# mLSTM by head with transposed scores: running maxima in rows through DRAM, denominators from ones columns, and a PSUM bank for each map's scores

## The chip, the cores and the metric

The kernel runs on one core of a Trainium2 chip. The metric is the device time of one execution in microseconds, and lower is better. Before the change the median of three runs is 1639.16 us (1638.51 to 1639.63).

## What is computed

One layer of an encoder for 272 tokens (16 meta tokens and 256 of input) with 2048 channels, in float32. One projection of the normalised input feeds three mixers (a short gated convolution A, an mLSTM of 4 heads B, a differential attention of 4 heads C) and their gates; the gated sum is projected and added to the input; a convolutional feed-forward block of 5632 channels follows. The change touches B and C only. The mLSTM, cut to what matters (q, k and v have 256 channels a head):

```python
b = jnp.cumsum(lfc, axis=-1)                        # log forget gates, summed
D = b[..., :, None] - b[..., None, :] + lic[..., None, :]
D = jnp.where(tri, D, -jnp.inf)
inter = b + m[..., None]
m_t = jnp.maximum(jnp.max(D, axis=-1), inter)       # running maximum
w = jnp.exp(D - m_t[..., None])
s = jnp.einsum('bhtd,bhsd->bhts', qc, kc) * w
num = g[..., None] * jnp.einsum('bhed,bhtd->bhte', C, qc) + jnp.einsum('bhts,bhse->bhte', s, vc)
den = g * jnp.einsum('bhd,bhtd->bht', n, qc) + jnp.sum(s, axis=-1)
h = num / jnp.maximum(jnp.abs(den), jnp.exp(-m_t))[..., None]
```

Both kernels compute it without chunks, as one causal map of 272 keys by 258 queries for each head. After it each head is RMS-normalised, scaled by a sigmoid gate, and projected. The differential attention takes, for each head, two softmax maps of 64 channels each and subtracts one from the other.

## The kernel before, in words

All large products are one **stream**: 537 slabs of 8 weight blocks (128x128) each come from DRAM in a fixed order (`Stream`). SyncE loads a slab into one of 5 raw buffers, ScalarE rounds it to `w_hi` (L187), VectorE makes the rest `w_lo` (L188), and TensorE multiplies each block three times (L273 to L275, called stream matmuls here). The split pair has 4 buffers; the split runs 3 slabs ahead of TensorE (`ahead=3`).

Everything else is **background**: generators that are advanced by one step (to their next `yield`) at each slab, which is a **tick**. The order in which engines get the instructions comes from the program's order and a scheduler's list; each engine then takes them in order. The background of differential attention is `diff_gen` (one generator a head), that of the mLSTM is `gates_gen` (once) and `ml_gen` (one a head and a query tile).

`QTILES` cuts the queries into tiles of 2, 128 and 128 (i = 0, 1, 2), which see 16, 144 and 272 keys. `KTILES` cuts the keys into 16, 128 and 128, `DTILES` into 100, 86 and 86. `ml_gen` makes, for one tile, the log weights of all keys by a matmul that selects the head's row from `crow` (L686), the scores with queries on the partitions (L689), maximum and mask in one VectorE instruction, the exponential on ScalarE, the product with its row sum, a transposition of the weighted scores to keys (L423), the product with v in three float32r matmuls a key tile (L710 to L712), and the transposition of the normalised result (L723). v itself is transposed to tokens at L433. `gates_gen` makes the gate columns (L632, L633, L639), the log sigmoid on [128, 12] tiles, and the running sums by matmuls with constant matrices (L666, L669, L674). `diff_gen` makes the scores at L484: the first map reads partitions 0 to 63, the second 64 to 127; the two maps of tile 2 have a bank each, those of tiles 1 and 0 share one bank (`shared`). Its other matmuls are L515, L525 and L537.

A float32 matmul stands in the trace as two records (two passes); a transposition and a float32r matmul as one.

Of the kernel before, what the change touches and what calls it, by code (L numbers as in the profile page):

```python
# [10 lines left out]
F32 = mybir.dt.float32  # L11
# [55 lines left out]
def _constants():  # L67
# [6 lines left out]
    for i, (q0, nq, nk) in enumerate(QTILES):  # L74
        t = q0 + np.arange(nq)[:, None]
        s = np.arange(nk)[None, :]
        put(f"mlm{i}", np.concatenate([np.zeros((nq, 1)), np.where(s <= t, 0.0, NEG)], 1).astype(np.float32))
        cid = lambda a: np.where(a < NMETA, 0, 1 + (a - NMETA) // 64)
        put(f"dam{i}", np.where(cid(s) <= cid(t), 0.0, NEG).astype(np.float32))
        for k, (k0, n) in enumerate(KTILES):  # L80
            if k0 >= nk:
                continue
            tt = k0 + np.arange(n)[:, None]
            ss = np.arange(-1, nk)[None, :]
            a = (tt <= ORIGIN[i]).astype(np.float32) - (tt <= ss).astype(np.float32)
            put(f"nt{i}_{k}", a)
    sel = np.zeros((NH, NH, 128), np.float32)
    for h in range(NH):
        sel[h, h] = 1.0
    put("sel", sel.reshape(NH, -1))  # L90
# [5 lines left out]
for _n, _w in (("g_mix", KT), ("g_ffn", KT), ("g_f", KT), ("conv_a", 12), ("ml_norm", 8), ("da_norm", 1),  # L96
               ("conv_f", 3 * FT), ("conv_fb", FT), ("b_if", 8), ("lam", 256)):
# [107 lines left out]
def encoder_layer_kernel(ctx: ExitStack, tc, xT, wst, wif, vecs, eye, consts, outT):  # L205
# [29 lines left out]
    nact = [1]  # L235
# [174 lines left out]
    def token_copy(v3, n, dst, lo=None):  # L410

        for a, b in ((slice(0, 16), slice(0, 1)), (slice(0, P), slice(1, n)))[: 1 if n == 1 else 2]:
            S.copy(dst[a, b], v3[a, b])
            if lo is not None:
                V.tensor_tensor(lo[a, b], v3[a, b], dst[a, b].bitcast(F32), op=ALU.subtract)

    def transpose_keys(src, nk, nq, dst, lo=None):

        ps = bank()
        n = 0  # L420
        for j, (k0, m) in enumerate(KTILES):
            if k0 < nk:
                T.transpose(ps[:m, j * P : j * P + nq], src[:nq, k0 : k0 + m], ident[:nq, :nq])  # L423
                n += 1
        v3 = ps[:, 0 : 3 * P].rearrange("p (j q) -> p j q", j=3)
        token_copy(v3[:, :, :nq], n, dst[:, :, :nq], None if lo is None else lo[:, :, :nq])
        return n

    def to_tokens(src, dst, lo=None):

        ps = bank()
        for j, (k0, m) in enumerate(KTILES):
            T.transpose(ps[:m, j * P : (j + 1) * P], src[:, k0 : k0 + m], ident)  # L433
        token_copy(ps[:, 0 : 3 * P].rearrange("p (j q) -> p j q", j=3), 3, dst, lo)

# [12 lines left out]
    def dv_put(vt, h):  # L448
# [4 lines left out]
        key_copy(dv[h], ps, 1)  # L453

# [15 lines left out]
    def diff_gen(h):  # L470
# [150 lines left out]
    lif = mix.tile([P, 3, 8], F32, name="lif")  # L621
    crow = [mix.tile([NH, 1 + q[2]], F32, name=f"crow{i}") for i, q in enumerate(QTILES)]
    nb = mix.tile([P, 3, NH], F32, name="nb")

    def gates_gen():
        split(wif2[:, :, 0:8], wif2[:, :, 8:16], wif_raw)
        V.tensor_tensor(eye2, ident[:16, 0:8], ident[:16, 8:16], op=ALU.add)
        V.memset(lif, 0.0)
# [8 lines left out]
        ps = bank()  # L637
        for j, (k0, m) in enumerate(KTILES):
            T.matmul(ps[:m, 8 * j : 8 * j + 8], lr[:, k0 : k0 + m], eye2, start=True, stop=True)  # L639
            V.tensor_tensor(lif[:m, j, :], ps[:m, 8 * j : 8 * j + 8], vs("b_if", 0, 8)[:m], op=ALU.add)  # L640
        f = lif[:, :, 4:8]
        y = small.tile([P, 3, 4], F32, tag="lsy", name="lsy")
        z = small.tile([P, 3, 4], F32, tag="lsz", name="lsz")
        z2 = small.tile([P, 3, 4], F32, tag="lsz2", name="lsz2")
# [284 lines left out]
```

## Time and profile before

| | before |
|---|---|
| median of 3 runs | 1639.16 us (1638.51 to 1639.63) |
| profiled execution, its own time | 1639.1 us |
| its span, first to last instruction | 1637.3 us |
| TensorE matmul busy | 99% of the span, 11948 records |
| VectorE busy | 62% |
| ScalarE busy | 45% |
| DMA | 53% of sixteen engines, 178 GB/s |

The span leaves 1.8 us around it. The busy times of the profile overlap where instructions are pipelined, so a TensorE instruction's own duration is its latency; what it costs the stream is read from the starts in the timeline.

### The profile page before, as it was taken

What the parts mean: (1) busy time and instruction counts of PE and PEld (TensorE: products, weight loads), DVE (VectorE), ACT (ScalarE), POOL (GpSimd) and SP (SyncE); (2) the same over time, 40 slices, a digit from 0 to 9 for tenths busy, and PEclk for the clock granted to TensorE, in tenths of its full rate; (3) what the DMA queues carried; (4) which work ended last, traced back from release to release, by engine and by line L of the source; (5) the groups of instructions that cost most, each with busy time, mean ns of one, the idle gap of its engine ahead of it and who ended that gap; (6) DMA issues with size and microseconds to landing.
All of it is one profiled execution on the core that took longest, in us unless ns stands there. A gap on an engine that the chain in (4) does not pass through costs nothing.

```text
span 1637.3 us, 29082 instructions
## 1 busy us (share of the span) xinstructions
PE 1618.4 (99%) x11948; PEld 1535.6 (94%) x11948; DVE 1007.7 (62%) x1594; ACT 738.4 (45%) x1067; POOL 46.6 (3%) x53
## 2 busy tenths in 40 slices
PE   8999999999999999999999999999999999999997
PEld 8999999899999999999999999999889999999886
DVE  6566555555555655656666777766556677676554
ACT  6445434344455544444444444444333444444442
POOL 0000000000000000000110000000000000000121
PEclk9999999999999999999999999999999999999998
DMA  8444555444444455555665555555555555555552
GB/s 318 150 155 146 179 181 181 146 151 155 142 147 150 160 183 192 185 181 180 201 207 177 181 189 183 185 189 182 192 185 189 181 185 188 183 188 183 191 183 90
DMA packets 83974, 291.03 MB, mean 178 GB/s; under 512 B 9344, under 2 KB 14080, under 8 KB 83712
## 3 DMA queue, kind: packets, MB, share of 16 engines
q1 hardware_dynamic: 82448, 287.91, 53.0%
q8 instruction: 93, 1.52, 0.4%
q10 hardware_dynamic: 1392, 1.26, 0.2%
q14 instruction: 41, 0.34, 0.1%
HBM read 287.03 MB, written 2.10 MB: 177 GB/s over the span
## 4 chain that ended last, share of the span: by engine, by line
PE 98%; issue 1%; DVE 0%; DMA 0%; ACT 0%; POOL 0%; POOLq 0%; ACTq 0%; DVEq 0%
PE ps L273 22%; PE ps L274 22%; PE ps L275 21%; PE ps L289 20%; PE ps L290 10%; PE ps L689 0%; PE ps L484 0%; PE ps L710 0%; PE ps L525 0%; PE ps L686 0%; DVE h L885 0%; DMA x_sb<-in_xT 0%; PE ps L515 0%; PE ps L712 0%; PE ps L711 0%
## 5 line engine op out<-in xcount | busy, mean ns | idle before, releaser
L187 ACT CAST w_hi<-w_raw 128x1024 fp32r<-128x1024 f32 (+1 forms) x537 | 562.7, 1048 | 813.8 <-issue 316.3
L188 DVE TENSOR_TENSOR w_lo<-w_raw,w_hi 128x1024 fp32r<-128x1024 f32 (+1 forms) x537 | 656.2, 1222 | 429.8 <-ACT w_hi L187 426.1
L273 PE MATMUL ps<-uhl,w_hi 128*128 128x258 f32 (+2 forms) x1664 | 482.2, 290 | 7.1 <-ACT w_hi L187 7.1
L274 PE MATMUL ps<-uhl,w_hi 128*128 128x258 f32 (+2 forms) x1664 | 476.3, 286 | 0.0
L275 PE MATMUL ps<-uhl,w_lo 128*128 128x258 f32 (+2 forms) x1664 | 473.5, 285 | 0.0
L273 PEld LDWEIGHTS ps<-uhl,w_hi 128*128 128x128 f32 x1664 | 314.3, 189 | 9.5 <-ACT w_hi L187 7.1
L274 PEld LDWEIGHTS ps<-uhl,w_hi 128*128 128x128 f32 x1664 | 315.6, 190 | 0.7
L275 PEld LDWEIGHTS ps<-uhl,w_lo 128*128 128x128 f32 x1664 | 314.4, 189 | 0.3
L289 PE MATMUL ps<-fhl,w_hi 128*128 128x512 f32 x704 | 252.2, 397 | 0.0
L289 PE MATMUL ps<-act,w_hi 128*128 128x512 f32 x682 | 237.5, 394 | 0.0
L274 PE MATMUL ps<-fhl,w_hi 128*128 128x258 f32 x704 | 199.7, 284 | 0.0
L273 PE MATMUL ps<-fhl,w_hi 128*128 128x258 f32 x704 | 198.8, 282 | 0.0
L275 PE MATMUL ps<-fhl,w_lo 128*128 128x258 f32 x704 | 197.5, 280 | 0.0
L290 PE MATMUL ps<-fhl,w_lo 128*128 128x256 f32 x704 | 189.9, 280 | 0.0
L290 PE MATMUL ps<-act,w_lo 128*128 128x256 f32 x682 | 187.6, 282 | 0.0
L289 PEld LDWEIGHTS ps<-fhl,w_hi 128*128 128x128 f32 x704 | 132.4, 188 | 28.3
L289 PEld LDWEIGHTS ps<-act,w_hi 128*128 128x128 f32 x682 | 126.1, 188 | 26.9
L274 PEld LDWEIGHTS ps<-fhl,w_hi 128*128 128x128 f32 x704 | 133.2, 189 | 2.1
L290 PEld LDWEIGHTS ps<-fhl,w_lo 128*128 128x128 f32 x704 | 133.2, 189 | 1.8
L275 PEld LDWEIGHTS ps<-fhl,w_lo 128*128 128x128 f32 x704 | 134.2, 191 | 0.0
L273 PEld LDWEIGHTS ps<-fhl,w_hi 128*128 128x128 f32 x704 | 132.4, 188 | 0.0
L290 PEld LDWEIGHTS ps<-act,w_lo 128*128 128x128 f32 x682 | 128.2, 188 | 3.0
(233 smaller groups left out, 1555.8 us busy)
## 6 DMA issues: line engine op xcount, KB each, us to landing
w_raw<-in_wst SPq DMA_DIRECT2D x535, 512.0 KB, 3.3
xr<-in_xT SPq DMA_DIRECT2D x16, 129.0 KB, 3.8
x_sb<-in_xT SPq DMA_DIRECT2D x7, 272.0 KB, 6.6
cst<-in_consts SPq DMA_DIRECT2D x1, 1252.5 KB, 6.6
out<-h SPq DMA_DIRECT2D x4, 256.0 KB, 3.1
out<-h ACTq DMA_DIRECT2D x3, 256.0 KB, 3.2
w_raw<-in_wst SPq DMA_DIRECT2D x2, 256.0 KB, 4.8
x_sb<-in_xT ACTq DMA_DIRECT2D x2, 136.0 KB, 3.1
```

The lines of the kernel that those rows point to most:

```text
L187: self.nc.scalar.copy(hi[:, a], raw[:, a])
L188: self.nc.vector.tensor_tensor(lo[:, a], raw[:, a], hi.bitcast(F32)[:, a], op=ALU.subtract)
L273: T.matmul(o, wh, xh[:, k, c0:c1], start=start, stop=False)
L274: T.matmul(o, wh, xl[:, k, c0:c1], start=False, stop=False)
L275: T.matmul(o, wl, xh[:, k, c0:c1], start=False, stop=stop)
L289: one = lambda: T.matmul(o, wh, xhl[:, k, :, a:b], start=(k == 0), stop=(k == K - 1))
L290: two = lambda: T.matmul(o[:, : b - a], wl, xhl[:, k, 0, a:b], start=False, stop=False)
```

## The change

- **Gates in rows.** `gates_gen` keeps the gates of the four heads as rows [4, 272]: two matmuls (L635, L636 of the changed kernel), the log sigmoid on [4, 272] tiles, the running sum and the running maximum by doubling steps on VectorE. Three rows go to DRAM from ScalarE's queue (`crow`, `nrow`, `erow`) and come back: as columns `ccol` and `ecol` (one element a packet), and per head as `w`, a row broadcast to 128 partitions.
- **mLSTM by head.** `ml_gen` runs once a head. The scores are made transposed, keys on the partitions, in three key tiles of 100, 86 and 86 (`DTILES`); only queries from 0, 86 and 172 on are made for them. So the transposition of weighted scores goes. The result is made in three query tiles of 86 (`MQ`), from 1, 2 and 3 key tiles. v has two more columns (ones in the high part), whose product is the denominator.
- **v and the result.** Both halves of a head's v are transposed in one step (`mv_evac`), and so is the result of all queries.
- **Differential attention.** The two maps of a head have a bank each for all three query tiles, and the six score matmuls are issued one after the other, before the first VectorE instruction on them.
- **Order of the background.** One generator runs at a time (`nact` is gone).

```diff
-        ("mlm0", 17), ("mlm1", 145), ("mlm2", 273),
-        ("dam0", 16), ("dam1", 144), ("dam2", 272),
-        ("nt0_0", 17), ("nt1_0", 145), ("nt1_1", 145),
-        ("nt2_0", 273), ("nt2_1", 273), ("nt2_2", 273),
-        ("sel", NH * 128),
+        ("dam0", 16), ("dam1", 144), ("dam2", 272), ("causal", PW),
...
     def tick():
...
-            i = 0
-            g = background[i]
-            background.remove(g)
+            g = background.popleft()
             try:
                 next(g)
-                background.insert(min(nact[0] - 1, len(background)), g)
+                background.appendleft(g)
...
+    def mv_evac(h, j):
...
+                for ks in ((0,), (1, 2)):
+                    m = DTILES[ks[0]][1]
+                    ps = bank()
+                    for n, k in enumerate(ks):
+                        for i in range(2):
+                            c = n * 256 + i * P
+                            T.transpose(ps[:m, c : c + P], vt[:, i, DTILES[k][0] : DTILES[k][0] + m], ident)
...
+                    split(hi, lo, src)
...
     def diff_gen(h):
-        pm = {}
-        shared = None
+        pm, sc = {}, {}
+        pair, col = [bank(), bank()], 0
         for i, (q0, nq, nk) in reversed(list(enumerate(QTILES))):
             a = q0 - SKIP
-            if i < 2 and shared is None:
-                shared = bank()
             for m in range(2):
-                ps = bank() if i == 2 else shared[:, 2 * NMETA + 144 * m :] if i else shared[:, NMETA * m :]
+                ps = pair[m][:, col : col + nk]
                 r = slice(64 * m, 64 * m + 64)
                 T.matmul(ps[:nq, :nk], dq[h][r, a : a + nq], dk[h][r, :nk], start=True, stop=True)
+                sc[i, m] = ps
+            col += nk
+        for i, (q0, nq, nk) in reversed(list(enumerate(QTILES))):
+            for m in range(2):
+                ps = sc[i, m]
...
     def gates_gen():
...
+        T.matmul(pf[:NH, :TOK], eye2[:, 4:8], lr, start=True, stop=True)
+        T.matmul(ps[:NH, :TOK], eye2[:, 0:4], lr, start=True, stop=True)
...
+        while d <= P:
+            V.tensor_tensor(two[:, lo], one[:, lo], one[:, d : MID + d], op=ALU.add)
+            V.tensor_tensor(two[:, hi], one[:, hi], one[:, MID + P - d : MID + 2 * P - d], op=ALU.add)
...
+        S.dma_start(crow, c)
...
+        while d <= TOK:
+            V.tensor_tensor(b[:, PADN:], a[:, PADN:], a[:, PADN - d : PADN + 1 + TOK - d], op=ALU.max)
...
+        S.activation(e[:, :TQ], e[:, :TQ], AF.Exp)
+        S.dma_start(nrow, nm)
+        S.dma_start(erow, e[:, :TQ])
+        yield
+        yield
+        for k, (k0, m) in enumerate(DTILES):
+            S.dma_start(ccol[:m, k, :], crow[:, k0 : k0 + m].rearrange("h p -> p h"))
+            S.dma_start(ecol[:MQ, k, :], erow[:, k * MQ : (k + 1) * MQ].rearrange("h p -> p h"))
...
-    def ml_gen(h, i):
...
+    def ml_gen(h):
+        w = mwork.tile([P, PW], F32, tag="p0", name="w")
+        S.dma_start(w, nrow[h : h + 1, :].broadcast_to([P, PW]))
+        yield from rest(2)
+        seg = [slice(PCOL[k], PCOL[k] + TQ - k * MQ) for k in range(3)]
+        V.tensor_tensor(w, w, cc("causal"), op=ALU.add)
+        for k, (k0, m) in enumerate(DTILES):
+            S.activation(w[:m, seg[k]], w[:m, seg[k]], AF.Exp, bias=ccol[:m, k, h : h + 1])
+        sc = [bank(), bank()]
+        for k, (k0, m) in enumerate(DTILES):
+            o = sc[0][:m, :TQ] if k == 0 else sc[1][:m, PCOL[k] - TQ : seg[k].stop - TQ]
+            for j in range(2):
+                T.matmul(o, kh[h][:, j, k0 : k0 + m], qh[h][:, j, k * MQ :], start=(j == 0), stop=(j == 1))
...
+        for n, m in enumerate((DTILES[0][1], DTILES[1][1])):
+            r = slice(n * TQ, (n + 1) * TQ)
+            V.scalar_tensor_tensor(w[:m, r], sc[n][:m, :TQ], 1.0 / 16, w[:m, r], op0=ALU.mult, op1=ALU.mult)
+            split(sh[:m, r], sl[:m, r], w[:m, r])
+        yield from rest(3)
...
+        for a in (2, 1, 0):
+            for k in range(a + 1):
+                m = DTILES[k][1]
+                c = PCOL[k] + (a - k) * MQ
+                sa, sb = sh[:m, c : c + MQ], sl[:m, c : c + MQ]
+                o = ps[a][:MQ, : 256 + 2]
+                T.matmul(o, sa, va[:m, k, :], start=(k == 0), stop=False)
+                T.matmul(o, sa, vb[:m, k, :], start=False, stop=False)
+                T.matmul(o, sb, va[:m, k, :], start=False, stop=(k == a))
...
+            V.tensor_copy(t[:, a : a + 1], ps[a][:MQ, 256:257])
...
+            S.activation(hs[:MQ, a, :], ps[a][:MQ, :256], AF.Square, scale=r[:, a : a + 1], accum_out=ss[:, a : a + 1])
...
+        G.tensor_tensor(ss, t, nhalf[:MQ, 0:3], op=ALU.pow)
+        V.tensor_tensor(fac, ss, r, op=ALU.mult)
+        for a in (2, 1, 0):
+            S.activation(hs[:MQ, a, :], ps[a][:MQ, :256], AF.Copy, scale=fac[:, a : a + 1])
+        yield from rest(3)
...
+                T.transpose(ps[j][:, a * MQ : (a + 1) * MQ], hs[:MQ, a, j * P : (j + 1) * P], ident[:MQ, :MQ])
...
-        for i in (2, 1, 0):
-            later(lambda h=h, i=i: background.append(mark(("m", h, i), ml_gen(h, i))))
+        later(lambda h=h: background.append(mark(("m", h), ml_gen(h))))
```

What the change moves, at three places. The first is TensorE in the differential attention of head 0, behind the row that issues the first three score matmuls (`dqk` is the tile of q and k; a row with x2 stands for two equal instructions). Before:

```order
386 L275 MATMUL ps<-uhl,w_lo 128x272
387 L484 MATMUL ps<-dqk 128x144
388 L273 MATMUL ps<-uhl,w_hi 128x272
389 L274 MATMUL ps<-uhl,w_hi 128x272
390 L275 MATMUL ps<-uhl,w_lo 128x272
391 L273 MATMUL ps<-uhl,w_hi 128x272
392 L484 MATMUL ps<-dqk 2x16
393 L274 MATMUL ps<-uhl,w_hi 128x272
```

After the change, all six in a row:

```order
368 L265 MATMUL ps<-uhl,w_hi 128x272
369 L266 MATMUL ps<-uhl,w_lo 128x272
370 L473 MATMUL ps<-dqk 128x272 x2
371 L473 MATMUL ps<-dqk 128x144 x2
372 L473 MATMUL ps<-dqk 2x16 x2
373 L264 MATMUL ps<-uhl,w_hi 128x272
374 L265 MATMUL ps<-uhl,w_hi 128x272
```

Four separate places among the stream matmuls have become one, and equal sizes of the two maps stand side by side.

The second is TensorE in the mLSTM of head 0. Before, the scores of query tile 2 (tiles 1 and 0 come later, each with its own L686):

```order
2634 L274 MATMUL ps<-uhl,w_hi 128x258
2635 L275 MATMUL ps<-uhl,w_lo 128x258
2636 L686 MATMUL ps<-crow_3385,cst 128x273
2637 L689 MATMUL ps<-kh_3388,qh_3387 128x272 x2
2638 L273 MATMUL ps<-uhl,w_hi 128x258
2639 L274 MATMUL ps<-uhl,w_hi 128x258
```

After, the scores of the whole head:

```order
2660 L265 MATMUL ps<-uhl,w_hi 128x258
2661 L266 MATMUL ps<-uhl,w_lo 128x258
2662 L723 MATMUL ps<-qh_3389,kh_3390 100x258 x2
2663 L723 MATMUL ps<-qh_3389,kh_3390 86x172 x2
2664 L723 MATMUL ps<-qh_3389,kh_3390 86x86 x2
2665 L264 MATMUL ps<-uhl,w_hi 128x258
```

The matmul that spread `crow` is gone; three places a head have become one.

The third is ScalarE between the gates and the first head. Before, nothing stands there but slab roundings and the rounding of v:

```order
142 L647 ACT_TABLE_LOAD
143 L647 ACTIVATE lsy<-lsy 128x12
144 L187 CAST w_hi<-w_raw 128x1024 x9
145 L413 CAST vh_3391<-ps 16x128
146 L413 CAST vh_3391<-ps 128x2x128
```

After, the transfers to and from DRAM stand in the same queue (`g_...` are the row tiles of `gates_gen`):

```order
150 L181 CAST w_hi<-w_raw 128x1024 x8
151 L677 DMA crow<-g_p_3514 4x272
152 L181 CAST w_hi<-w_raw 128x1024
153 L706 DMA ccol<-crow 100x4x1
154 L706 DMA ccol<-crow 86x4x1 x2
155 L181 CAST w_hi<-w_raw 128x1024 x2
156 L287 CAST v0h<-ps 100x256
157 L287 CAST v0h<-ps 86x2x256
158 L701 DMA nrow<-g_nm 4x516
159 L700 ACTIVATE g_ax<-g_ax 4x258
160 L181 CAST w_hi<-w_raw 128x1024
161 L702 DMA erow<-g_ax 4x258
```

Behind them come the transfers of `ecol` and of `w`, with four more slab roundings between them, and then the first exponential, which reads `w` and `ccol`: six slab roundings stand between the issue of `ccol` and its reader.

## Rows read from the trace of the kernel before

**Rows 1.** The profile's page: busy time and share of each engine; the chain that ended last, by engine; and from the groups of instructions the two of the slab split (count | busy us, mean ns of one | idle us of the engine before them, and what ended it).

```profile
PE 1618.4 (99%) x11948; PEld 1535.6 (94%) x11948; DVE 1007.7 (62%) x1594; ACT 738.4 (45%) x1067; POOL 46.6 (3%) x53
...
PE 98%; issue 1%; DVE 0%; DMA 0%; ACT 0%; POOL 0%; POOLq 0%; ACTq 0%; DVEq 0%
...
L187 ACT CAST w_hi<-w_raw 128x1024 fp32r<-128x1024 f32 (+1 forms) x537 | 562.7, 1048 | 813.8 <-issue 316.3
L188 DVE TENSOR_TENSOR w_lo<-w_raw,w_hi 128x1024 fp32r<-128x1024 f32 (+1 forms) x537 | 656.2, 1222 | 429.8 <-ACT w_hi L187 426.1
```

**Rows 2.** Timeline of TensorE, two stream matmuls that are 24 apart (one slab); the second is the last one ahead of the first piece of group 3. Columns here and in groups 3 to 8: start us, duration us, engine, line, operation, tiles, shape, count merged.

```profile
348.00 0.28 PE L275 MATMUL ps<-uhl,w_lo 128*128 128x258 f32 x1
...
350.90 0.28 PE L275 MATMUL ps<-uhl,w_lo 128*128 128x258 f32 x1
```

**Rows 3.** Timeline of TensorE, the score pieces of the mLSTM's head 0 (query tiles 2, 1 and 0): of each its first line (and L689 of the first) and the second stream matmul behind it.

```profile
351.12 0.72 PE L686 MATMUL ps<-crow,cst 4*128 4x273 f32 x2
351.77 1.19 PE L689 MATMUL ps<-kh,qh 128*128 128x272 f32 x4
...
352.91 0.28 PE L274 MATMUL ps<-uhl,w_hi 128*128 128x258 f32 x1
...
355.78 0.51 PE L686 MATMUL ps<-crow,cst 4*128 4x145 f32 x2
...
356.93 0.28 PE L274 MATMUL ps<-uhl,w_hi 128*128 128x258 f32 x1
...
381.31 0.20 PE L686 MATMUL ps<-crow,cst 4*2 4x17 f32 x2
...
381.85 0.29 PE L274 MATMUL ps<-uhl,w_hi 128*128 128x272 f32 x1
```

**Rows 4.** Timeline of TensorE, the product with v of head 0 (tiles 2, 1 and 0; 9, 6 and 3 matmuls): the first matmul of each and the second stream matmul behind it.

```profile
366.26 0.38 PE L710 MATMUL ps<-vh,sh 16*128 16x256 f32 x1
...
367.74 0.29 PE L274 MATMUL ps<-uhl,w_hi 128*128 128x272 f32 x1
...
370.70 0.38 PE L710 MATMUL ps<-vh,sh 16*128 16x256 f32 x1
...
371.83 0.29 PE L274 MATMUL ps<-uhl,w_hi 128*128 128x272 f32 x1
...
391.52 0.27 PE L710 MATMUL ps<-vh,sh 16*2 16x256 f32 x1
...
392.17 0.28 PE L274 MATMUL ps<-uhl,w_hi 128*128 128x258 f32 x1
```

**Rows 5.** Timeline of TensorE, two pieces of transpositions of head 0 (weighted scores of tile 2; result of tile 0, which has 2 queries), each with the second stream matmul behind it.

```profile
359.71 0.49 PE L423 MATMUL ps<-ident,w 128*16 128x128 f32 x3
...
360.16 0.28 PE L274 MATMUL ps<-uhl,w_hi 128*128 128x258 f32 x1
...
398.27 0.28 PE L723 MATMUL ps<-ident,hsq 2*128 2x2 f32 x2
...
398.70 0.28 PE L274 MATMUL ps<-uhl,w_hi 128*128 128x258 f32 x1
```

**Rows 6.** Timeline of TensorE, pieces of the gates: one of three L639 pieces, and the pieces of the running sums of tiles 1 and 2, each with the second stream matmul behind it.

```profile
300.18 0.38 PE L639 MATMUL ps<-eye,lr 16*128 16x8 f32 x2
...
300.71 0.29 PE L274 MATMUL ps<-uhl,w_hi 128*128 128x258 f32 x1
...
318.81 0.74 PE L666 MATMUL ps<-cst,lif 16*4 16x145 f32 x4
...
320.69 0.29 PE L274 MATMUL ps<-uhl,w_hi 128*128 128x272 f32 x1
...
323.68 1.63 PE L666 MATMUL ps<-cst,lif 16*4 16x273 f32 x6
...
326.89 0.29 PE L274 MATMUL ps<-uhl,w_hi 128*128 128x272 f32 x1
```

**Rows 7.** Timeline of TensorE, the score pieces of the differential attention's head 0 (the fourth piece is like the third), each with the second stream matmul behind it.

```profile
56.98 0.97 PE L484 MATMUL ps<-dqk 64*128 64x272 f32 x6
...
58.11 0.29 PE L274 MATMUL ps<-uhl,w_hi 128*128 128x272 f32 x1
...
59.98 0.51 PE L484 MATMUL ps<-dqk 64*128 64x144 f32 x2
...
60.65 0.28 PE L274 MATMUL ps<-uhl,w_hi 128*128 128x272 f32 x1
...
61.12 0.20 PE L484 MATMUL ps<-dqk 64*2 64x16 f32 x2
...
61.48 0.29 PE L275 MATMUL ps<-uhl,w_lo 128*128 128x272 f32 x1
```

**Rows 8.** Timeline of TensorE, the product with v of the differential attention's head 0 and the transposition of its result; three squares, a power on GpSimd and three scaled copies stand between them.

```profile
78.41 1.50 PE L525 MATMUL ps<-dva,aT 100*128 100x128 f32 x12
...
85.82 0.49 PE L537 MATMUL ps<-ident,os 128*128 128x128 f32 x3
```

**Rows 9.** VectorE: from the groups by line and shape the one instruction on rows of 272 elements; and the stretch of the gates, 290 to 335 us (stretch, length, busy us and count of TensorE matmul, weight load, VectorE, ScalarE, GpSimd, granted TensorE clock, DMA share, GB/s).

```profile
L635 DVE TENSOR_TENSOR lr<-ps,R 16x272 f32<-16x272 f32 x1 | 0.4, 429 | 1.7 <-PE ps L633 1.7
...
290.00:335.00 45.00, 45.00 (x352) 40.72 (x351) 22.24 (x52) 13.69 (x15) 0.00 (x0) 1.00 0.43 140
```

**Rows 10.** The profile's page, DMA queues (packets, MB, share of sixteen engines): ScalarE's queue.

```profile
q10 hardware_dynamic: 1392, 1.26, 0.2%
```

More of the change, by code (lines that the diff above doesn't have):

```diff
@@ L76, in _constants @@
         s = np.arange(nk)[None, :]
-        put(f"mlm{i}", np.concatenate([np.zeros((nq, 1)), np.where(s <= t, 0.0, NEG)], 1).astype(np.float32))
         cid = lambda a: np.where(a < NMETA, 0, 1 + (a - NMETA) // 64)
         put(f"dam{i}", np.where(cid(s) <= cid(t), 0.0, NEG).astype(np.float32))
[L80 to L90, printed above, removed]
+    for k, (k0, n) in enumerate(DTILES):
+        t = np.arange(SKIP if k == 0 else k0, TOK)
+        a = np.full((P, t.size), NEG)
+        a[:n] = np.where(k0 + np.arange(n)[:, None] <= t[None, :], 0.0, NEG)
+        o = COFF["causal"][0] + PCOL[k]
+        c[:, o : o + t.size] = a
     return c
@@ L620, in encoder_layer_kernel @@
     S.dma_start(wif_raw, wif)
-    lif = mix.tile([P, 3, 8], F32, name="lif")
-    crow = [mix.tile([NH, 1 + q[2]], F32, name=f"crow{i}") for i, q in enumerate(QTILES)]
-    nb = mix.tile([P, 3, NH], F32, name="nb")
+    ccol = mix.tile([P, 3, NH], F32, name="ccol")
+    ecol = mix.tile([P, 3, NH], F32, name="ecol")
+    dram = mixl.enter_context(tc.tile_pool(name="dram", bufs=1, space=bass.MemoryType.DRAM))
+    nrow = dram.tile([NH, PW], F32, name="nrow")
+    crow = dram.tile([NH, TOK], F32, name="crow")
+    erow = dram.tile([NH, TQ], F32, name="erow")
+    PADN = 2 * P
     def gates_gen():
@@ L636, in gates_gen @@
         yield
[L637 to L644, printed above, removed]
+        ps, pf = bank(), bank()
+        T.matmul(pf[:NH, :TOK], eye2[:, 4:8], lr, start=True, stop=True)
+        T.matmul(ps[:NH, :TOK], eye2[:, 0:4], lr, start=True, stop=True)
+        t4 = lambda tag, n=TOK: mwork.tile([NH, n], F32, tag=tag, name="g_" + tag)
+        c, f, y, z, z2 = (t4(n) for n in ("p1", "p1", "ax", "pa", "ya"))
+        V.tensor_scalar(f, pf[:NH, :TOK], vs("b_if", 1)[:NH], None, op0=ALU.add)
+        V.tensor_scalar(c, ps[:NH, :TOK], vs("b_if", 0)[:NH], None, op0=ALU.add)
         V.tensor_scalar(z, f, -1.0, None, op0=ALU.mult)
@@ new lines, in gates_gen @@
+        lo, hi = slice(0, MID), slice(MID + P, MID + 2 * P)
+        one, two = (t4("p0", MID + 2 * P) for _ in range(2))
+        for t in (one, two):
+            V.memset(t, 0.0)
+        V.tensor_copy(one[:, lo], f[:, :MID])
+        V.tensor_scalar(one[:, hi], f[:, MID:], -1.0, None, op0=ALU.mult)
+        d = 1
+        while d <= P:
+            V.tensor_tensor(two[:, lo], one[:, lo], one[:, d : MID + d], op=ALU.add)
+            V.tensor_tensor(two[:, hi], one[:, hi], one[:, MID + P - d : MID + 2 * P - d], op=ALU.add)
+            one, two = two, one
+            d *= 2
+            if d == 8:
+                yield
@@ new lines, in gates_gen @@
+        mx = a[:, PADN + 1 + SKIP :]
+        nm = mwork.tile([NH, PW], F32, tag="hs", name="g_nm", bufs=1)
+        V.tensor_scalar(nm[:, :TQ], mx, -1.0, None, op0=ALU.mult)
+        for k in (1, 2):
+            V.tensor_copy(nm[:, PCOL[k] : PCOL[k] + TQ - k * MQ], nm[:, k * MQ : TQ])
+        e = y
+        n = MID - SKIP
+        V.tensor_tensor(e[:, :n], one[:, SKIP + 1 : MID + 1], nm[:, :n], op=ALU.add)
+        V.tensor_tensor(e[:, n:TQ], one[:, hi], nm[:, n:TQ], op=ALU.add)
+        yield
@@ L729, in ml_gen, with ones_columns @@
             ym["l"] = ymp.tile([P, 8, TQ], F32R, tag="y1", name="yml")
-        ymh, yml = ym["h"], ym["l"]
-        split(ymh[:, 2 * h : 2 * h + 2, a : a + nq], yml[:, 2 * h : 2 * h + 2, a : a + nq], y[:, :, :nq])
+        ps = [bank(), bank()]
+        for j in range(2):
+            for a in range(3):
+                T.transpose(ps[j][:, a * MQ : (a + 1) * MQ], hs[:MQ, a, j * P : (j + 1) * P], ident[:MQ, :MQ])
+        for j in range(2):
+            y = mwork.tile([P, TQ], F32, tag="p1", name="ymt")
+            V.tensor_tensor(y, ps[j][:, :TQ], soh[h][:, j, :], op=ALU.mult)
+            split(ym["h"][:, 2 * h + j, :], ym["l"][:, 2 * h + j, :], y)
+    vhs = [[mix.tile([P, 3, 256 + 2], F32R, name=f"v{j}{n}") for n in "hl"] for j in range(2)]
+    def ones_columns():
+        c = small.tile([P, 2, 6], F32, tag="oc", name="oc", bufs=1)
+        V.memset(c[:, 0, :], 1.0)
+        V.memset(c[:, 1, :], 0.0)
+        for v in vhs:
+            for n, t in enumerate(v):
+                S.copy(t[:, :, 256:], c[:, n, :].rearrange("p (k e) -> p k e", k=3))
     qk_sb = [(mix.tile([P, 4, TQ], F32, tag=f"m{2 * j}", name=f"qh{j}"),
@@ L739, in encoder_layer_kernel @@
         if h > 1:
-            drain(("m", h - 2, 0))
+            drain(("m", h - 2))
         qh[h], kh[h] = (t[:, 2 * (h % 2) : 2 * (h % 2) + 2, :] for t in qk_sb[h // 2])
-        vh[h] = [mix.tile([P, 3, 256], F32R, tag=f"vh{j}", name=f"vh{h}{j}", bufs=2) for j in range(2)]
+        vh[h] = vhs[h % 2]
         soh[h] = mix.tile([P, 2, TQ], F32, tag="so", name=f"so{h}", bufs=2)
```

140 lines of the change are left out of this document (50 added, 90 removed).

## The prediction

> **What bounds the kernel now.** I read the page first: TensorE is busy for 99% of the span and makes 98% of the chain that ended last [rows 1]. The reader should then look at the slab split. ScalarE's rounding is idle for 814 us in front of its 537 instructions and VectorE's rest waits only for ScalarE [rows 1]: the split is held by full buffers, so it stands at its limit of 3 slabs ahead. A slab lasts TensorE 2.90 us for 24 stream matmuls, 0.121 us each [rows 2]; the lead is therefore 8.7 us. So TensorE's own instruction time sets the end. The change leaves the stream alone, and its worth is what the background costs TensorE before and after, unless TensorE is made to wait.
>
> Matmuls overlap, so I price a piece of background by starts: from its first start to the second stream matmul behind it, less one stream matmul (0.12). Where the piece uses fewer rows of the array than the stream (4, 16 or 64), the last stream matmul ahead lies 0.22 us before it instead of 0.12 [rows 2, 3], so 0.10 is added.
>
> **What goes, by head 0 (heads are alike; four of them).** Scores with L686: 1.77, 1.13 and 0.52 us [rows 3], 3.42 a head, 13.7 in all. Product with v: 1.46, 1.11 and 0.63 [rows 4], 3.20 a head, 12.8. Transposition of weighted scores: three cost 0.33, so 0.11 each [rows 5]; with two for tile 1 and about 0.3 for the 2-row one, 0.85 a head, 3.4. Transposition of the result: 0.22 twice and 0.41 [rows 5], 0.85 a head, 3.4. Gates: the three L639 pieces at 0.51, 0.51 and an estimated 0.3, the running sums at 3.19, 1.86 and an estimated 0.4 [rows 6], 6.75. Differential scores: 1.11, 0.65 and twice 0.34 [rows 7], 2.44 a head, 9.8.
>
> **What comes.** The first two score pieces are six passes each and differ by 0.64 us for 128 or 129 columns [rows 3]: 0.107 a pass, 0.83 ns a column; 0.3 us is left over, which is the change of row count on the way in and from L686 to L689.
>
> *Scores.* Per head four passes each of 258, 172 and 86 columns, all with 128 rows, so without that 0.3: 0.86 + 0.57 + 0.29 = 1.72. The trace has no pass of 86 columns on 86 weights. It could be held by its weight load; a transposition with 128 columns takes 0.11 [rows 5], and at 0.11 the last term is 0.44. With a little for the way out I take 1.85 (1.72 to 1.97), 7.4 in all: saves 6.3.
>
> *Product with v.* 18 matmuls of 258 columns a head in place of 18 of 256. The stream's 0.121 for 258 columns is the nearest row; contraction over 100 and 86 rows is of the kind that L525 has. 2.16 a head (0.108 to 0.125 each), 8.6 in all: saves 4.2. What it saves is the change from 16 rows to 128 and back, in each of three pieces.
>
> *Transpositions.* Those of the weighted scores go: 3.4. The result takes 6 a head of 86 columns each; by column they are 0.07, by the nearest row 0.11, which I take: 2.6, saves 0.8 (up to 1.7). v stays at 6 a head: nothing.
>
> *Gates.* L635 and L636 are four passes of 272 columns (0.23 each) with 0.4 for the row change: 1.3, saves 5.4.
>
> *Differential scores.* The first piece holds four passes of 272 and two of 144 columns in a duration of 0.97 us [rows 7]. One after the other these would be 4 x 0.23 + 2 x 0.12 = 1.16, so the two maps' large passes ran side by side: 0.46 + 0.24 = 0.70, and 0.41 is entry and exit. After, the 144 passes are side by side too, in two banks: 0.46 + 0.24 + 0.1 for the small pair + 0.4 = 1.2 a head, 4.8 in all: saves 5.0. If pairs ran in turn it would be 2.0 a head: saves 1.8.
>
> Sum: 6.3 + 4.2 + 3.4 + 0.8 + 5.4 + 5.0 = 25.1 us. The profiled execution took 1639.1 us (span 1637.3), level with the median 1639.16, so 1614.0. With all bounds one way: 1611.5 to 1618.3.
>
> **What I cost at nothing, and its cover.** VectorE gains some 40 gate instructions on rows of 258 to 273 elements, at 0.43 us the nearest row [rows 9], and 20 on about half: 17 + 6 = 23 us, where the old gates took some 6. In 290 to 335 us it is busy for 22.2 of 45 [rows 9], so it would be 39 of 45. Behind these stand slab rests; the lead of 8.7 us covers a bunch of about 20 of them (some 6 us). ScalarE has the DMAs of the third order block: each holds the slab roundings queued behind it until the row that it reads has landed. It rounds a slab in 1.05 us of each 2.90 [rows 1], so the same lead covers a hold. SyncE's and GpSimd's queues lose or gain nothing that counts.
>
> The columns `ccol` are 1088 packets of one element. ScalarE's queue has moved 1392 packets in 0.2% of sixteen engines' span [rows 10]: 52 us, 38 ns each. Spread over sixteen engines that is 2.6 us; all on one engine, 41 us. Six slabs, 17.4 us, stand between the issue and the first reader, and the lead adds 8.7: 26 us before TensorE waits. I take no wait, since a spread over two engines (21 us) already suffices.
> The Trainium skill's DMA: Bandwidth & Descriptors (sections "Why a DMA increments its semaphore by 16 and not by 1" and "Specifications") says that such a transfer runs on the largest number of engines up to 16 that divides both sides' slowest dimensions, and that pieces under 512 B miss line rate; it speaks against this change. By it the 86-row columns get two engines, and the sum would stay as it is by the row's 38 ns; no run here shows it yet.
>
> **The rivals.**
> - *TensorE waits for the slower chains.* Between the product with v and the transposition of the result, the differential attention has 7.4 us, 1.3 of them matmuls [rows 8], for three squares, a power and three copies of 128 columns. The mLSTM now has three ticks, 8.7 us, but 256 columns and six more small VectorE instructions, some 2 us more: 8 of 8.7. One us late in each head, plus 2 to 4 us once if the gates overrun the lead: 3 to 8 us, so 1617 to 1622. For it: both margins are thin. Against it: VectorE and ScalarE have slack on the average.
> - *The maps don't run side by side in the new order* (that the banks don't do what they say): 3.2 us less gain, 1617.2. Against it, the 0.97 us of rows 7, for the same pair.
> - *The columns land late, and the kernel gets slower.* One place: the first exponential of head 0 holds ScalarE, and slab roundings behind it stop. If one engine carries all 1088 packets at 38 ns, TensorE waits 41 - 26 = 15 us: 1629. From 0.05 us a packet the wait exceeds the 25 us gained; at 0.06 it is 39 us, 1653. The same rule of the skill stands beside this; by its two engines the place would need twice that price. For it: no row shows one-element packets. Against it, the spread has to fail altogether.
>
> **How the numbers follow.** Likeliest, no new wait and pairs side by side: 0.70, at 1614.0 (1611.5 to 1618.3). Waits for the chains: 0.18, 1617 to 1622. Pairs in turn: 0.08, 1617.2. Columns late: 0.04, mostly slower. A measurement of this kernel tells 0.2% (3.3 us) from no change. Faster by more than that are the first three and a little of the last, less 0.02 in which several waits fall together and eat most of the gain: 0.94; within 0.02, slower 0.04. The range 1611 to 1622 leaves out the late columns and the far ends: some 2 in 10.
>
> **What would show it.** TensorE still 99% busy, its records down, no wait of TensorE above a microsecond between 290 and 560 us. One score piece a head of about 1.85 us; a product with v of 2.16 us without gaps above 0.13 between starts; six equal transpositions at 0.11; one differential score piece of 1.2 us with both maps' starts a few ns apart. Wrong would be: TensorE waits with VectorE or ScalarE named in front of L764, L739 or the first slabs after the gates; ScalarE held in front of L718; `ccol` landing later than 17 us.

## The result and the profile after

| | before | after |
|---|---|---|
| median | 1639.09 us (1638.51 to 1639.63) | 1614.55 us (1614.41 to 1615.72) |
| ratio to before, 95% interval | | 0.9852 (0.9835 to 0.9869) |
| profiled execution, its own time | 1639.1 us | 1614.41 us |
| its span | 1637.3 us | 1612.6 us |

The changed kernel is 24.5 us faster. The forecast was 1614.0 in a range from 1611 to 1622.

The page of the changed kernel, the lines that answer to those of before (the split stands at L181 and L182 now; the second line is ScalarE's DMA queue):

```profile
PE 1593.6 (99%) x11862; PEld 1524.1 (95%) x11862; DVE 1007.6 (62%) x1524; ACT 722.1 (45%) x1028; POOL 43.3 (3%) x45
...
q10 hardware_dynamic: 4132, 2.34, 0.5%
...
PE 98%; issue 1%; DVE 0%; DMA 0%; ACT 0%; SPq 0%; POOLq 0%; POOL 0%; DVEq 0%; ACTq 0%
...
L182 DVE TENSOR_TENSOR w_lo<-w_raw,w_hi 128x1024 fp32r<-128x1024 f32 (+1 forms) x537 | 656.1, 1222 | 433.4 <-ACT w_hi L181 431.7
L181 ACT CAST w_hi<-w_raw 128x1024 fp32r<-128x1024 f32 (+1 forms) x537 | 562.7, 1048 | 795.8 <-issue 303.8
```

Nothing has changed in what bounds it: TensorE is busy for 99% and makes 98% of the chain, as in [rows 1]; it has 86 records fewer. All that it waited for, over the whole span (waits of TensorE; total us, times, longest):

```profile
PE ps L264 <- ACT w_hi L181: 7.2, 1, 7.2
PE ps L928 <- DVE dg L927: 1.5, 1, 1.5
PE ps L921 <- ACT sq L901: 0.9, 1, 0.9
```

These are the start, the normalisation and the tail; nothing that the change added stands among them. So the gain has to lie in the pieces of background. Timeline of TensorE after the change, each piece and the second stream matmul behind it:

```profile
56.85 1.11 PE L473 MATMUL ps<-dqk 64*128 64x272 f32 x12
...
58.12 0.28 PE L265 MATMUL ps<-uhl,w_hi 128*128 128x272 f32 x1
...
293.72 0.62 PE L635 MATMUL ps<-lr,eye 16*4 16x272 f32 x2
...
294.95 0.28 PE L265 MATMUL ps<-uhl,w_hi 128*128 128x258 f32 x1
...
345.88 1.92 PE L723 MATMUL ps<-qh,kh 128*100 128x258 f32 x12
...
347.80 0.28 PE L265 MATMUL ps<-uhl,w_hi 128*128 128x258 f32 x1
...
356.63 0.28 PE L739 MATMUL ps<-v0h,sh 100*86 100x258 f32 x1
...
358.93 0.29 PE L265 MATMUL ps<-uhl,w_hi 128*128 128x272 f32 x1
...
367.89 0.61 PE L764 MATMUL ps<-ident,hs 86*128 86x86 f32 x6
...
368.51 0.29 PE L265 MATMUL ps<-uhl,w_hi 128*128 128x272 f32 x1
```

Priced as in the prediction (difference of the two starts, less 0.12, plus 0.1 where few rows are used) these are 1.25, 1.21, 1.80, 2.18 and 0.50 us. Over all heads, from the exact starts of both traces:

| pieces, us in all | before | after | saved | forecast |
|---|---|---|---|---|
| scores of the mLSTM | 13.57 | 7.18 | 6.4 | 6.3 |
| product with v | 12.91 | 8.65 | 4.3 | 4.2 |
| transposition of weighted scores | 3.34 | 0 | 3.3 | 3.4 |
| transposition of the result | 3.48 | 1.96 | 1.5 | 0.8 |
| gates | 6.77 | 1.20 | 5.6 | 5.4 |
| scores of the differential attention | 9.66 | 4.94 | 4.7 | 5.0 |
| transposition in the differential attention | 3.07 | 2.63 | 0.4 | 0 |
| sum | | | 26.2 | 25.1 |

The span fell by 24.7 us, so about 1.5 us of the 26.2 came back elsewhere (below).

### The profile page after: what moved, and what is told of

Same layout as the page of the kernel before. It is cut to its first block, busy times and chain, and to the rows that moved or that the text cites. A ratio compares the mean times of both kernels' runs of the same rounds, so it can differ in the third digit from the quotient of the medians.

```text
span 1612.6 us, 28802 instructions
## 1 busy us (share of the span) xinstructions
PE 1593.6 (99%) x11862; PEld 1524.1 (95%) x11862; DVE 1007.6 (62%) x1524; ACT 722.1 (45%) x1028; POOL 43.3 (3%) x45
## 4 chain that ended last, share of the span: by engine, by line
PE 98%; issue 1%; DVE 0%; DMA 0%; ACT 0%; SPq 0%; POOLq 0%; POOL 0%; DVEq 0%; ACTq 0%
PE ps L265 22%; PE ps L264 22%; PE ps L266 22%; PE ps L280 20%; PE ps L281 10%; PE ps L723 0%; PE ps L519 0%; DMA w_raw<-in_wst 0%; DVE h L932 0%; PE ps L473 0%; PE ps L739 0%; PE ps L741 0%; PE ps L740 0%; PE ps L434 0%; PE ps L509 0%
## 5 line engine op out<-in xcount | busy, mean ns | idle before, releaser
L182 DVE TENSOR_TENSOR w_lo<-w_raw,w_hi 128x1024 fp32r<-128x1024 f32 (+1 forms) x537 | 656.1, 1222 | 433.4 <-ACT w_hi L181 431.7
L181 ACT CAST w_hi<-w_raw 128x1024 fp32r<-128x1024 f32 (+1 forms) x537 | 562.7, 1048 | 795.8 <-issue 303.8
```

The source lines that it names most:

```text
L181: self.nc.scalar.copy(hi[:, a], raw[:, a])
L182: self.nc.vector.tensor_tensor(lo[:, a], raw[:, a], hi.bitcast(F32)[:, a], op=ALU.subtract)
```

## The experiments

Most of these kernels differ from the changed kernel by a few microseconds. They are judged by their pieces on TensorE first, and the time of each stands beside.

**One part alone.** The kernel before, with the new `diff_gen` scores (the loop over `pair`) and nothing else.

```diff
-                ps = bank() if i == 2 else shared[:, 2 * NMETA + 144 * m :] if i else shared[:, NMETA * m :]
+                ps = pair[m][:, col : col + nk]
```

> The kernel before with one part of the change alone: the two maps of the differential attention have a bank each, and the six score matmuls of a head stand in a row. Theory (what the change saves is the sum of its pieces on TensorE, and the maps run side by side in the new order): the score pieces go from 2.42 to 1.24 us a head as in the changed kernel, and the wait of 0.23 us for the two-row tile in two heads goes, so 4.7 to 5.2 us less: 1634.2 us. Rival (the pairs run in turn once they stand in a row, and the gain of the changed kernel comes from elsewhere): 2.0 us a head, 1.8 us less, 1637.4.

Measured: 1633.95 us (1633.07 to 1634.11), 4.7 below the 1638.67 of before on that chip, ratio 0.997 (0.9958 to 0.9981). The score piece takes 1.24 us a head, and the transposition behind it 2.63 in all in place of 3.07: the wait for the two-row tile `d0`, which was in two heads of before, goes with this part. The theory holds; the rival's 1637.4 is out.

**The order within the piece.** The same six matmuls in a row and the same two banks, one map after the other.

```diff
-        for i, (q0, nq, nk) in reversed(list(enumerate(QTILES))):
-            for m in range(2):
+        for m in range(2):
+            for i, (q0, nq, nk) in reversed(list(enumerate(QTILES))):
...
```

> The changed kernel, but with the differential scores map by map: 272, 144 and 16 columns of the first map, then the three of the second; still six in a row, still a bank for each map. Theory (a pair of matmuls on partitions 0 to 63 and 64 to 127 runs side by side only when neighbours differ in their half): a head's piece goes from 1.24 to about 2.0 us, 3 us in all, 1617.6. Rival (one entry and exit in place of four is the whole gain, and the order within the piece is without effect): 1614.5, unchanged.

Measured: 1619.07 us (1618.76 to 1619.42), 4.5 more than the changed kernel: the way that the theory said, and more than its 3. Timeline of TensorE, the piece of head 0 and the second stream matmul behind it:

```profile
56.54 2.12 PE L474 MATMUL ps<-dqk 64*128 64x272 f32 x12
...
58.83 0.29 PE L265 MATMUL ps<-uhl,w_hi 128*128 128x272 f32 x1
```

The twelve passes last 2.12 us where they lasted 1.11; the piece is 2.25 us a head, 4.06 in all. In the exact starts of the changed kernel the two maps' passes begin 6 to 7 ns apart; here each begins behind the one before. So here the maps run side by side only when neighbours read different halves, and putting the matmuls in a row is worth little by itself: in turn, 2.25 of the former 2.42 would have stayed.

**Six places for two.** The scores of a head at three places, a slab apart, and its product with v at three.

```diff
+            if k:
+                yield
             o = sc[0][:m, :TQ] if k == 0 else ...
...
+            if a < 2:
+                yield
             for k in range(a + 1):
```

> The changed kernel, but the scores of a head of the mLSTM stand at three places (one for each key tile, a slab apart) in place of one, and its product with v at three places in place of one: four more places a head, the same instructions. Theory (what a place cost before was the change of row count, and here all pieces use 86 to 128 rows): at most 0.05 us a place, 0.8 us in all, 1614.5 to 1615.5. Rival (every place among the stream matmuls costs its own 0.3 us, as the pieces of before had over their columns): 16 places, 4.8 us more, 1619.4.

Measured: 1614.52 us (1614.32 to 1615.08), level with the changed kernel. The pieces sum to 7.17 us (scores) and 8.69 (product), to be held against 7.18 and 8.65. A place among the stream matmuls costs nothing here. What the pieces of [rows 3] and [rows 4] had over their columns was not the number of places; the rival falls.

**What a change costs.** Added matmuls that nobody reads, each at its own place, two passes of 64 columns; only rows and weights differ. In the first kernel all have 64 weights, in the second most have 128.

```diff
+        for kk in ((4, 16, 64, 128)[h], (32, 48, 80, 100)[h]):
+            yield
+            T.matmul(bank()[:64, :64], ident[:kk, :64], ident[:kk, :64], start=True, stop=True)
...
```

> The changed kernel with two added matmuls a head, each at a place of its own a slab apart, between the product with v and the transposition of the result: float32, 64 columns on 64 weights, nobody reads the result. Only the number of rows that they contract over differs: 4 and 32 in head 0, 16 and 48 in head 1, 64 and 80 in head 2, 128 and 100 in head 3. By the 0.83 ns a column, 64 columns in two passes are 0.11 us. Theory (a change of the row count costs about 0.3 us a place): 0.4 to 0.5 us for 4, 16, 32 and 64 rows, 0.1 to 0.2 for 100 and 128; 48 and 80 lie at one of the two. Rival (a piece costs its columns and a fixed entry, whatever its rows): all eight alike.

Measured: all eight pieces 0.45 us, from 4 rows to 128 (one run, 1617.95 us). As it stood, that was the rival's result. But the 64 weights were the same in all eight and had not been varied, so the second kernel varied both:

> Again two added matmuls a head, each at its own place, float32, 64 columns, result read by nobody; this time rows x weights are 4x128 and 32x128 in head 0, 16x128 and 64x128 in head 1, 80x128 and 128x128 in head 2, 128x64 and 128x80 in head 3 (with 64 weights all row counts had cost the same 0.45 us). Theory (the change costs its 0.3 us where the rows or the weights are 64 or fewer): 0.4 to 0.5 us for 4, 16, 32 and 64 rows and for 128x64; 0.1 to 0.2 for 80x128, 128x128 and 128x80. Rival (only the number of weights counts): 0.1 to 0.2 for all but 128x64. Rival (any small float32 piece costs it): all eight 0.45.

Measured (one run, 1616.98 us): 0.556 us for 4, 16, 32 and 64 rows on 128 weights; 0.224 for 80x128 and 0.222 for 128x128; 0.448 for 128x64; 0.179 for 128x80. Timeline of TensorE, four of them (the shape behind the tiles is rows * weights) with the second stream matmul behind each:

```profile
418.21 0.43 PE L759 MATMUL ps<-ident 64*128 64x64 f32 x2
...
418.81 0.29 PE L265 MATMUL ps<-uhl,w_hi 128*128 128x272 f32 x1
...
468.22 0.33 PE L759 MATMUL ps<-ident 80*128 80x64 f32 x2
...
468.57 0.29 PE L265 MATMUL ps<-uhl,w_hi 128*128 128x272 f32 x1
...
520.91 0.33 PE L759 MATMUL ps<-ident 128*64 128x64 f32 x2
...
521.40 0.28 PE L265 MATMUL ps<-ydl,w_hi 128*128 128x258 f32 x1
...
524.17 0.29 PE L759 MATMUL ps<-ident 128*80 128x64 f32 x2
...
524.48 0.28 PE L265 MATMUL ps<-uhl,w_hi 128*128 128x258 f32 x1
```

Between 80 and 64 rows 0.33 us are added, between 80 and 64 weights 0.27. It is 64 or fewer rows, or 64 weights, that cost, and both rivals fall. In the exact starts 0.09 of the 0.33 us lie in front of the piece, 0.10 between its two passes and 0.14 behind it; so the price is paid on the way in, at the first pass and on the way out. The eight pieces sum to 3.3 us and the one run is 2.4 longer; 0.9 us of the difference had arisen before 63 us, where the two kernels are alike. The Trainium skill's TensorEngine Tiling (Array Packing), section "Key Properties", says that changing the tiling mode drains the engine, and its "Overview" calls dimensions of 64 or less small, for which the array can be made into smaller tiles. The trace agrees with that size, as 80 is free of the price and 64 is not, and it gives the price, 0.33 and 0.27 us; that the engine drains is not to be seen in it as such.

**The chain behind the product.** Fewer slabs between the product with v and the transposition of its result, another number in each head.

```diff
-        yield from rest(3)
+        yield from rest(3 - h)
```

> The changed kernel, but the transposition of the mLSTM's result follows the product with v after 3, 2, 1 and 0 slabs in heads 0, 1, 2 and 3 (3 in all heads of the changed kernel). Theory (by the changed kernel's trace the chain of square, power and copies takes 5.25 us from the end of the last product to the last copy): no wait after 2 slabs (5.8 us), about 2.6 us of TensorE waiting after 1, about 5.5 us after 0; 8 us in all, 1622.6. Rival (the 8 us that the prediction gave the chain): 2.2, 5.1 and 8 us, 15 in all, 1630.

In the changed kernel the product of head 0 ends its starts at 358.68; then (operations on `hs`, the normalised result; duration min/median/max, first and last start):

```profile
L764 PE MATMUL ps<-ident,hs x6: 235/237/238, 367.9 to 368.3; 86*128 86x86 f32 x6
L751 ACT ACTIVATE hs<-ps,st x3: 457/461/470, 360.1 to 361.1; 86x256 f32<-86x256 f32 x3
...
L756 ACT ACTIVATE hs<-ps,st x3: 458/463/470, 363.0 to 363.7; 86x256 f32<-86x256 f32 x3
```

The last copy ends at 364.2, TensorE reads it at 367.9: 3.7 us to spare. Measured with fewer slabs: 1619.17 us, 4.6 more. Waits of TensorE between 460 and 530 us:

```profile
PE ps L764 <- ACT hs L756: 3.4, 2, 2.2
```

No wait in heads 0 and 1. The order that came out had 31 and 24 stream matmuls between product and transposition in heads 2 and 3 (the scheduler left more than the 24 and 0 asked for), and the pieces grew by 1.4 and 2.8 us: 31 x 0.12 + 1.4 and 24 x 0.12 + 2.4 (the standstill alone, by starts) are 5.1 and 5.3. The chain is 5.1 to 5.3 us long, as the theory said; the prediction's 8 is out. The theory's 1622.6 was not reached because the slabs left out were fewer than asked for.

A second price came with it. Windows of head 2 behind its wait of 1.2 us, then of head 3 in its wait of 2.2 us and behind it (columns as in [rows 9]):

```profile
468.70:472.00 3.30, 3.30 (x29) 3.30 (x30) 2.88 (x6) 2.17 (x4) 0.00 (x0) 1.00 0.00 0
...
519.90:522.30 2.40, 0.24 (x2) 0.03 (x1) 0.49 (x2) 1.20 (x4) 0.84 (x1) 1.00 0.04 14
522.60:525.90 3.30, 3.30 (x19) 3.30 (x18) 2.66 (x5) 1.65 (x4) 0.00 (x0) 0.50 0.02 5
526.20:529.00 2.80, 2.80 (x25) 2.80 (x24) 1.21 (x3) 1.05 (x1) 0.00 (x0) 1.00 0.43 162
```

After 2.2 us of waiting the granted clock stood at 0.50 (the 1.2 GHz level) for 3.4 us, and stream matmuls were 0.215 us apart in place of 0.121, twelve of them: some 1.1 us that no wait shows, beside the slower transpositions that are in the 2.8. After head 2's 1.2 us it stayed at 1.00.

**The columns.** Every one-element transfer issued twice.

```diff
+            for cd, ed in ((ccol2, ecol2), (ccol, ecol)):
-            S.dma_start(ccol[:m, k, :], crow[:, k0 : k0 + m].rearrange("h p -> p h"))
+                S.dma_start(cd[:m, k, :], crow[:, k0 : k0 + m].rearrange("h p -> p h"))
...
```

> The changed kernel with each of the six column transfers (one element a packet) issued twice, the first time into tiles that nobody reads. Theory (what the columns cost is that ScalarE stands still while it issues them, 2.3 to 2.9 us for each from the third on): the three of the second group become six and hold ScalarE for about 14 us in place of 5.8, head 0 comes 8 us later, and as its weighted scores are ready 4.9 us before TensorE uses them, TensorE waits about 3 us in front of the first product with v (2 to 5 us more, 1617 to 1619.5). Rival (only the landing counts, and the issue is cheap): no wait, 1614.5. The price of 38 ns a packet on one engine, from the prediction: 2176 packets, 83 us, 57 us of wait.

ScalarE's queue, timeline of the changed kernel (issue of `ccol`, and of the last two `ecol`), with the slab rounding behind it:

```profile
321.98 3.05 ACTq L706 DMA_DIRECT2D ccol<-crow  x3
...
334.68 5.49 ACTq L707 DMA_DIRECT2D ecol<-erow  x2
340.20 1.05 ACT L181 CAST w_hi<-w_raw 128x1024 fp32r<-128x1024 f32 x1 [4.56 <-PE ps L265]
```

and with the transfers doubled:

```profile
321.81 7.89 ACTq L709 DMA_DIRECT2D ccol<-crow  x5
...
339.36 7.35 ACTq L710 DMA_DIRECT2D ecol<-erow  x4
346.75 1.04 ACT L181 CAST w_hi<-w_raw 128x1024 fp32r<-128x1024 f32 x1 [6.97 <-PE ps L726]
```

Measured: 1616.86 us (1616.78 to 1616.94), 2.3 more. New waits of TensorE are 0.2 (a slab's rounding) and 0.8 (a slab's rest) and, in front of the result's transposition of head 0:

```profile
PE ps L767 <- ACT hs L759: 0.9, 1, 0.9
```

The size is at the lower edge of the theory's; the place is not the theory's, since nothing waits in front of the product, and the doubled group of `ecol` held the queue for 8.8 us (from 337.93), not 14. The three new waits stand behind that group, none behind the doubled `ccol`. So the price of these transfers here is the standstill of the queue that issues them. Whether an issue itself takes that long, or is held because earlier packets have not been moved yet, no run tells. That they land is no concern: the whole of `ccol` moved from 322 to 329.5 us, and its reader came at 345.2. The queue's row for that stretch of the changed kernel:

```profile
q10 hardware_dynamic: 1102, 0.00, 8.2%
```

8.2% of sixteen engines over 7.5 us are 9.8 us for 1102 packets, 9 ns each.

**VectorE's gate work.** Each instruction of the running sum four times, then twice.

```diff
+            for _ in range(4):
-            V.tensor_tensor(two[:, lo], one[:, lo], one[:, d : MID + d], op=ALU.add)
+                V.tensor_tensor(two[:, lo], one[:, lo], one[:, d : MID + d], op=ALU.add)
...
```

> The changed kernel with every VectorE instruction of the gates' running sum issued four times (the same values again): 48 more instructions, 12.6 us by their rows, in one bunch, with one slab rest waiting behind it. Theory (VectorE's gate work costs nothing until a bunch has used up TensorE's lead, which is 7.5 us at this slab in the changed kernel): TensorE waits 12.6 - 7.5 = 5.1 us once, 1619.7. Rival (it is hidden whatever its size, as VectorE is busy for 62% only): 1614.5. Rival (it counts in full): 1627.

Measured: 1622.92 us (1621.41 to 1624.09), 8.4 more than the changed kernel. The one new wait, and four stretches around it (stretch, length, busy us and count of TensorE matmul, weight load, VectorE, ScalarE, GpSimd, granted TensorE clock, DMA share, GB/s):

```profile
PE ps L266 <- DVE w_lo L182: 6.1, 1, 6.1
```

```profile
319.00:325.30 6.30, 6.30 (x52) 6.30 (x51) 6.30 (x31) 2.12 (x3) 0.00 (x0) 1.00 0.00 1
...
325.30:331.60 6.30, 0.31 (x3) 0.11 (x1) 6.30 (x27) 1.04 (x1) 0.00 (x0) 0.91 0.00 1
...
331.60:337.00 5.40, 5.30 (x25) 5.28 (x25) 5.40 (x11) 0.38 (x1) 0.00 (x0) 0.50 0.69 199
...
337.00:345.00 8.00, 8.00 (x68) 8.00 (x67) 7.29 (x18) 4.13 (x6) 0.00 (x0) 0.98 0.71 245
```

The mechanism is the theory's; both its numbers were off. The lead was not 7.5: I had read the use of the slab behind. In the changed kernel the rest that stands behind the bunch, and TensorE's first use of it, are

```profile
320.02 1.21 DVE L182 TENSOR_TENSOR w_lo<-w_raw,w_hi 128x1024 fp32r<-128x1024 f32 x1
...
325.12 0.28 PE L266 MATMUL ps<-uhl,w_lo 128*128 128x258 f32 x1
```

that is, 3.9 us from its end to its use. And 48 instructions from start to start take 48 x 0.21 = 10.1 us, not 12.6. 10.1 - 3.9 = 6.2, measured 6.1. The profiled execution took 1624.09 us, 9.7 more than that of the changed kernel. Beside the wait, 2.5 of it came right behind: the granted clock stands at 0.50 (the 1.2 GHz level) for the next 5 us, where the stream matmuls are 0.215 us apart in place of 0.121, and the first 34 of them with the transposition of v among them take 7.3 us in place of 4.8. The last 1.1 us are not placed.

> The changed kernel with every VectorE instruction of the gates' running sum issued twice in place of four times: 16 more, at 0.21 us from start to start 3.4 us. Theory (a bunch costs nothing until the lead is used up; in the changed kernel the rest of the slab behind it ends at 321.2 and TensorE wants it at 325.2, so 4.0 us are left): no wait, 1614.6. Rival (the cost is in proportion to the work: 48 more instructions cost 8.4 us): 2.8 us, 1617.3.

Measured: 1614.72 us (1614.29 to 1615.15), and TensorE has the three waits of the changed kernel and no other. The rest behind the bunch:

```profile
322.38 1.21 DVE L182 TENSOR_TENSOR w_lo<-w_raw,w_hi 128x1024 fp32r<-128x1024 f32 x1
```

It ends at 323.59, and TensorE uses it at 324.12: still in time, by 0.5 us. (By the clock it comes 2.4 us later, but the stream of this execution is 1.0 ahead here, so 3.4 of the 3.9 are used up, as the theory had it.) Twice the work costs nothing, four times costs 8.4: a threshold, not a proportion.

**A try at something better.** If 64 or fewer weights cost a change, the two-query tile of the differential attention (2 weights) does.

```diff
-                T.matmul(ps[:nq, :nk], dq[h][r, a : a + nq], dk[h][r, :nk], start=True, stop=True)
+                T.matmul(ps[:P, :nk], dq[h][r, a : a + P], dk[h][r, :nk], start=True, stop=True)
```

> The changed kernel, but the two queries of tile 0 of the differential attention are loaded as 128 weights (the queries behind them go along, their scores are not read). Theory (2 weights cost a change of their own: the pair starts 0.21 us behind the last pass of 144 columns in place of 0.12): a head's piece goes from 1.24 to 1.05 to 1.15 us, 0.4 to 0.8 us in all, 1613.8 to 1614.2. Rival (128 weights take longer to load than 2, and that eats it): 1.24 us or more, 1614.5 to 1615.

Measured: 1614.30 us (1614.03 to 1614.52), piece 1.23 us in place of 1.24: no difference to the changed kernel. In the exact starts the small pair comes 0.12 us behind the last large pass, as the theory had it, but the next stream matmul follows its last pass after 0.19 us in place of 0.10. The saving is lost again at the exit, so the time is as the rival said; that it is the loading of more weights, as the rival had it, is not shown.

## Why the prediction was right

**What bounds it.** Right: TensorE's own time decided, and the sum of its pieces gave the time within 0.6 us. That it came so close is partly luck: the pieces saved 1.1 us more than the 25.1 of the sum, and some 1.5 us that the sum did not have came back.

**Terms.** Scores, product, gates and the weighted scores' transposition are within 0.2 us of their terms. Two were mis-sized. The result's transpositions cost 0.073 us each (six of 86 columns in a piece of 0.49), so the price goes by columns, and I had taken the 0.11 of [rows 5], which are 128 columns wide; that is 0.7 us more gain. The differential scores saved 0.3 less: 1.24 a head, not 1.2, and the pieces of before were 9.66, not 9.8. What the sum left out is the wait for `d0` (0.4 us), which goes with the differential attention's part alone; whether its banks or its order of instructions do it, no run tells apart.

**What a piece had over its columns.** I called it the change of row count. That is shown now, from both sides: more places at 86 to 128 rows add nothing, and 64 rows on 128 weights cost 0.33 us more than 80 do. The name was too wide in one way and too narrow in another: a change from 128 rows to 80, 86 or 100 is free, and 64 weights cost without any change of rows. The 0.3 us that the prediction has left over in the first two score pieces is 0.41 by its own price (1.77 less 1634 columns at 0.83 ns); the 0.10 added for the way in is missing from it, and no term of the sum hangs on that. It also says why 100, 86 and 86 keys are cheap where 16, 128 and 128 were not: no product with v leaves the full array any more.

**Pairs side by side.** The 0.97 us of [rows 7], from which I took it, was a sound reading. In turn it would have cost 4.5 us, not the 3.2 of that rival, as 2.25 us a head, not 2.0, is what the maps take in turn.

**Covered work.** VectorE's gate work was the thin place, as the rival said, and it did hold. In the changed kernel VectorE is busy for 38.2 of the 45 us of [rows 9], the forecast 39:

```profile
290.00:335.00 45.00, 45.00 (x361) 43.95 (x359) 38.22 (x86) 18.42 (x21) 0.00 (x0) 1.00 0.49 153
```

But 8.7 us of lead is the distance in slabs; from the end of a rest to its use about 7 us are there on other slabs, and 3.9 were left behind the bunch of the running sum. The other half of that rival was mis-sized on the safe side: 5.2 us of chain in place of 8. The 7.4 us of [rows 8] from which I worked it out are the distance at which the program sets the transposition, not the time that the chain needs. In the same trace of before, the copies that end the chain are

```profile
82.00 0.89 ACT L533 ACTIVATE os<-ps,ss 128x128 f32<-128x128 f32 x3 [1.17 <-POOL ss L531]
```

so the last one ended at 82.89, 2.9 us before TensorE read it at 85.82.

**Columns.** 38 ns a packet was four times too much. It came from a row whose packets were larger; 9 ns is the measured price of these. The Trainium skill's DMA: Bandwidth & Descriptors, section "Why a DMA increments its semaphore by 16 and not by 1", spoke against the transfer, as it gives it few engines; no run here shows on how many these packets ran. They landed 15 us before their reader. What they cost is the time of their issue, which the prediction did not price at all, and which the lead covered.

**What came back.** Of 26.2 us in pieces the span shows 24.7. Some 0.2 us lie in start and tail. Some 0.9 us are in the feed-forward block's last product, which from its first to its last matmul of 512 columns takes 491.0 us in place of 490.1 in the exact starts: a pair of its matmuls, of 512 and 256 columns, takes 352.4 ns from start to start in place of 350.8. The block's other pairs of these widths take 352.9 before and 353.0 after. The kernel with the maps' part alone has the 350.8 of before, those made from the changed kernel the 352.4 of after; why is open, no run here tells it. The last 0.4 us are not placed.

## What to carry to other kernels

Where TensorE is full, price background work by starts, not by durations, and look first at its shapes: here 64 or fewer rows, or 64 weights, cost some 0.3 us a piece, while one place more or less among matmuls of more than 64 rows and weights costs nothing. Two matmuls on different halves of the rows are worth setting next to each other. Here each had a bank of its own; both in one bank were not tried. Work on engines that are not the bound is free up to the lead and dear beyond it, so measure the lead from the end of the last preparing step to the first use. A chain's length is read from its first and last instruction, not from the place where the program sets its reader.

## What was not expected of the hardware

- The change of part costs by weights too: 128 rows on 64 weights 0.448 us, on 80 weights 0.179.
- Issuing a transfer of 344 or 400 one-element packets holds the issuing queue: 0.24 to 0.38 us for three of the six, 2.3 to 2.9 us for the third of `ccol` and the second and third of `ecol`.
- After TensorE had stood still for 6.1 us its granted clock was 0.50 for about 5 us, which cost 2.5 us on top. A wait of 2.2 us was followed by 3.4 us at 0.50, and one of 1.2 us by none.
